# The last third of a decoder layer rearranged: norm, projections and the last feed-forward block

## The chip, the cores and the metric

One core of a Trainium2 chip runs the program. The metric is the device time of one execution in microseconds (us). PE is the matrix engine, DVE, ACT and POOL are the engines that work on vectors, and SP only issues DMAs. Each of them takes its instructions in a fixed order.

## The reference

One layer over 2048 tokens with 1024 features: eight attention heads (three dilated patterns, merged by weights from their softmax sums) beside eight RWKV-7 heads, whose 1024 outputs meet in `w_out`; then a layer norm, a SwiGLU feed-forward net with 2816 hidden features, and a second layer norm.

```python
mix = jnp.concatenate([o_att, o_rw], axis=-1) @ w_out[l]
h = layer_norm(ALPHA * h + mix, ln_mix_g[l], ln_mix_b[l])

ffn = (jax.nn.silu(h @ w_ffn_gate[l]) * (h @ w_ffn_up[l])) @ w_ffn_down[l]
h = layer_norm(ALPHA * h + ffn, ln_ffn_g[l], ln_ffn_b[l])
```

`layer_norm` subtracts the mean, divides by the standard deviation, multiplies by a vector g over the features and adds a vector b.

## The kernel before

Three parts run one after the other: `recurrent` (RWKV), `attention`, and `tail` (everything in the four lines above). The change touches `tail` and the end of `attention`, the function `merge`.

**Precision.** Every matmul of the tail runs in three parts. `split` makes a rounded copy "h" of an operand on ACT (L143), and the remainder "l" by a subtraction on DVE or POOL (L149). PE then adds h·h, l·h and h·l, each one matmul of 128x128 by 128x512.

**Merge.** For head pair 3, the last one, `merge` forms the weighted sum of three patterns in four pieces Q of 512 tokens. For Q 0 and 1 PE spreads the weights, and DVE and POOL multiply (L962, L964). For Q 2 and 3 the weights come back from DRAM (tile `f`, loads issued by POOL at L948); POOL makes two of the products, DVE the third (L950) and the last addition (L968).

**Tail.** Tokens are in four blocks of 512, numbered 0 to 3.
- `mix` projects a block by `w_out`: 8 k-steps, each with a load of weights (`draw`), a load of the heads' outputs (`or`), their splits, and 3 matmuls for each 128-token tile and each half of the 1024 columns. A block costs 192 matmuls.
- `norm_mix` normalises a block with g and b on DVE and POOL and stores it to `z_d`; `transposed` turns it by PE transposes (32 a block, tiles `tp`), copies it by ACT (`ht`) and stores it to `h_d`.
- `operands(S)` loads two blocks back (`hr`), makes differences on POOL (L1136, 16 in all) and 28 splits: the right-hand operands of a Strassen scheme with seven products, B11 to B22 and T1 to T4.
- `up(S)` runs gate and up products for 1024 tokens: 1848 matmuls into PSUM tiles `y`; results go to `hid_d`.
- `down(B)` multiplies a block's hidden features (`hraw`) by `w_ffn_down` (`draw`): 22 k-steps, 528 matmuls. `finish` is the second norm and the store of `out`.

Before, all three inputs of `product` (`draw`, `or`, `hraw`) share four slots, and `graw`, `hr`, `T`, `ht` share four others. The 8 PSUM banks are one pool. The order of the work is `mix` of blocks 0 and 1 (k 4 to 7), then the rest of 0, the rest of 1, 2 and 3, `up(0)`, `down(0)`, `down(1)`, `up(1)`, `down(2)`, `down(3)`. A generator `beside` is advanced by one step after each k-step and so lays norms, transposes and operands between the matmuls; the Tile framework then fixes each engine's order. The last block runs its k-steps three times: token tiles 0 to 2, then tile 3's left half, then its right half, so `draw` is loaded and split again for tile 3.

Of the kernel before, what the change touches and what calls it, by code (L numbers as in the profile page):

```python
# [9 lines left out]
F32 = mybir.dt.float32  # L10
F32R = mybir.dt.float32r
# [94 lines left out]
FAST = True  # L106
MIXED = (1, 2)
LASTLOW = ("pool", "pool", "dve")
# [4 lines left out]
class Layer:  # L113
# [617 lines left out]
    def attention(self):  # L731
        nc, tc, io = self.nc, self.tc, self.io
        amask = self.cst("amask")
        with ExitStack() as es:
# [160 lines left out]
            def merge(hp, os_, stats):  # L895
# [43 lines left out]
                w4 = w.rearrange("p a (h n) -> p a h n", h=2)  # L939
                for Q in range(NQ):  # L940
                    cols = slice(Q * QT, (Q + 1) * QT)
                    us = []
                    for p in range(3):
                        u = fp.tile([128, QT], F32, name="u", bufs=3)
                        if hp < 3 or Q >= NPE:
                            f = fp.tile([128, QT], F32, name="f", bufs=6)
                            src = self.f_d[hp, p, :, cols]
                            nc.gpsimd.dma_start(f, bass.AP(tensor=src.tensor, offset=src.offset,  # L948
                                                           ap=[list(src.ap[0]), [0, 64], [1, QT]]))
                            (nc.vector if p == 2 and hp == 3 else nc.gpsimd).tensor_tensor(u, os_[p][:, cols], f, op=ALU.mult)  # L950
                        else:

                            g = ps_s.tile([128, 4, 128], F32, name="g", tag="s")
                            for n in range(4):
                                for h in range(2):
                                    nc.tensor.matmul(g[64 * h:64 * h + 64, n], w4[:, p, h, 4 * Q + n:4 * Q + n + 1].to_broadcast([128, 64]),
                                                     self.ident, start=True, stop=True)
                            g = g.rearrange("p a b -> p (a b)")
                            if p == 0:
                                f = fp.tile([128, QT], F32, name="f", bufs=6)  # L960
                                nc.scalar.copy(f, g)
                                nc.gpsimd.tensor_tensor(u, os_[p][:, cols], f, op=ALU.mult)  # L962
                            else:
                                nc.vector.tensor_tensor(u, os_[p][:, cols], g, op=ALU.mult)  # L964
                        us.append(u)
                    if hp < 3 or Q >= NPE:
# [15 lines left out]

    def norm(self, sp, t, g, b, eps, mexp, fast=False):

        nc = self.nc
        st = sp.tile([128, 2, 6], F32, name="st", bufs=4)
        for i in range(2):
            nc.vector.bn_stats(st[:, i], t[:, i * 512:(i + 1) * 512])
        mv = sp.tile([128, 2], F32, name="mv", bufs=4)
        nc.vector.bn_aggr(mv, st)  # L990
        rs = sp.tile([128, 1], F32, name="rs", bufs=4)
# [10 lines left out]
    def tail(self):  # L1002
# [9 lines left out]
        with ExitStack() as es:  # L1012
# [22 lines left out]
            def bank(name):  # L1035
                return ps.tile([128, 512], F32, name=name, tag="y")
# [263 lines left out]
```

## Time and profile before

| quantity | value |
|---|---|
| time, median of 3 runs | 3450.7 us (3448.55 to 3455.49) |
| time of the profiled execution | 3452.88 us |
| its span (first to last event) | 3451.1 us |
| granted clock of PE, mean over the span | 0.943 |
| PE busy | 3202.5 us, 93% |
| tail, from its first matmul at 1729.12 us | 1722.0 us |

The span runs from the first to the last recorded event. An engine's busy share says how much of that it worked; a wait row says which engine's result ended a wait. The tail is cut into six stages below: projections, `up(0)`, `down(0)` with `down(1)`, `up(1)`, `down(2)`, `down(3)` with the end.

### The profile page before, as it was taken

Reading aid. Unit: us, or ns where it says so; the run is one execution under the profiler, and the core shown is the slowest. Engines: PE = TensorE matmul, PEld = TensorE weight load, DVE = VectorE, ACT = ScalarE, POOL = GpSimd, SP = SyncE. Lnnn points to the kernel's source line nnn. Section 1 sums busy time; section 2 is a strip of 40 time slices with the busy share of each in tenths; the row PEclk is TensorE's granted clock in tenths of the full one; section 3 lists DMA queues with packets and bytes.
Section 4 is the critical chain, followed back from the end, with each engine's and each line's share of the span. In section 5 each row is a group of like instructions: output and inputs, shape, how many; then the busy total and the mean of one; then the engine's idle time right before and its main releaser. Section 6 shows DMA issues by size and latency. Waiting matters only on the chain.

```text
span 3451.1 us, 48043 instructions
## 1 busy us (share of the span) xinstructions
PE 3202.5 (93%) x16836; PEld 2549.9 (74%) x16836; DVE 1916.0 (56%) x3887; ACT 1261.5 (37%) x2892; POOL 1294.9 (38%) x1298
## 2 busy tenths in 40 slices
PE   8999999999999988999978679999899999999996
PEld 5677778777777876777766568888777788888774
DVE  3456556566565433666547855555735655554334
ACT  4443343333332324666423423333422232323233
POOL 4444444343333240044414643232524522221286
PEclk9999999899888899999989889999999999999998
DMA  5553343443432448553347542222544322224455
GB/s 148 145 131 97 86 121 100 107 107 98 107 99 78 114 132 195 119 142 105 119 127 261 201 147 86 80 80 84 204 139 147 116 98 79 80 80 153 132 189 174
DMA packets 420317, 431.79 MB, mean 125 GB/s; under 512 B 97833, under 2 KB 313513, under 8 KB 417002
## 3 DMA queue, kind: packets, MB, share of 16 engines
q1 hardware_dynamic: 396490, 413.16, 40.0%
q0 software_dynamic: 23584, 15.56, 1.7%
q8 instruction: 132, 2.16, 0.3%
q14 instruction: 111, 0.91, 0.1%
HBM read 329.49 MB, written 98.97 MB: 124 GB/s over the span
## 4 chain that ended last, share of the span: by engine, by line
PE 48%; DMA 9%; DVE 7%; POOL 3%; issue 3%; ACT 2%; SPq 0%; ACTq 0%; POOLq 0%; DVEq 0%
PE y L1185 8%; PE y L1183 8%; PE y L1184 8%; DMA hraw<-hid_d 4%; PE acc L852 3%; PE s L812 3%; PE t L834 2%; DVE wl L149 2%; PE acc L1065 2%; PE acc L1064 2%; PE acc L1063 2%; PE s L813 2%; PE yr L291 1%; ACT wh L143 1%; PE yr L292 1%
## 5 line engine op out<-in xcount | busy, mean ns | idle before, releaser
L149 POOL TENSOR_TENSOR wrl<-wraw,wrh 128x256 fp32r<-128x256 f32 x416 | 330.1, 798 | 507.3 <-ACT wrh L143 477.8
L291 PE MATMUL yr<-xh,wrh 128*128 128x512 f32 x832 | 363.3, 437 | 48.3 <-ACT xh L143 22.5
L149 DVE TENSOR_TENSOR wl<-draw,wh 128x512 fp32r<-128x512 f32 x209 | 200.4, 980 | 324.6 <-ACT wh L143 295.1
L292 PE MATMUL yr<-xl,wrh 128*128 128x512 f32 x832 | 349.9, 421 | 0.9 <-DVE xl L149 0.8
L293 PE MATMUL yr<-xh,wrl 128*128 128x512 f32 x832 | 349.6, 421 | 1.0 <-POOL wrl L149 0.5
L143 ACT CAST wrh<-wraw 128x256 fp32r<-128x256 f32 x416 | 166.1, 404 | 442.9 <-PE yr L292 279.0
L1064 PE MATMUL acc<-wh,p 128*128 128x512 f32 x656 | 264.5, 404 | 28.8 <-DVE p L149 22.2
L1065 PE MATMUL acc<-wl,p 128*128 128x512 f32 x656 | 263.4, 405 | 4.2 <-POOL wl L149 2.7
L1063 PE MATMUL acc<-wh,p 128*128 128x512 f32 x656 | 239.4, 405 | 20.9 <-ACT p L143 19.9
L143 ACT CAST wh<-draw 128x512 fp32r<-128x512 f32 x284 | 169.7, 619 | 206.7 <-PE acc L1064 67.8
L1169 POOL TENSOR_TENSOR S<-graw 128x512 f32<-128x512 f32 x44 | 58.1, 1320 | 493.1 <-DVE gl L149 447.3
L291 PEld LDWEIGHTS yr<-xh,wrh 128*128 128x128 f32 x832 | 169.1, 203 | 97.0 <-ACT xh L143 27.2
L143 ACT CAST gh<-graw 128x512 fp32r<-128x512 f32 x176 | 109.3, 621 | 305.1 <-PE y L1184 287.0
L817 ACT ACTIVATE e<-e,ml 128x256 f32<-128x256 f32 (+1 forms) x384 | 175.0, 457 | 92.5 <-DVE ml L815 88.9
L815 DVE CUSTOM_DVE_ANT_0 e<-s,c 128x256 f32<-128x256 f32 (+1 forms) x384 | 134.2, 363 | 130.9 <-PE s L813 114.5
L293 PEld LDWEIGHTS yr<-xh,wrl 128*128 128x128 f32 x832 | 167.3, 201 | 43.0 <-POOL wrl L149 5.6
L292 PEld LDWEIGHTS yr<-xl,wrh 128*128 128x128 f32 x832 | 168.3, 202 | 38.2 <-DVE xl L149 5.1
L149 POOL TENSOR_TENSOR p<-hraw,p 128x512 fp32r<-128x512 f32 x66 | 87.8, 1332 | 288.4 <-ACT p L143 288.4
L1064 PEld LDWEIGHTS acc<-wh,p 128*128 128x128 f32 x656 | 126.7, 193 | 64.6 <-DVE p L149 25.5
L143 ACT CAST gh<-S 128x512 fp32r<-128x512 f32 x132 | 82.1, 622 | 243.6 <-PE y L1184 230.7
L1063 PEld LDWEIGHTS acc<-wh,p 128*128 128x128 f32 x656 | 127.5, 196 | 51.0 <-ACT p L143 23.7
L812 PE MATMUL s<-kh,qs 128*128 128x256 f32 (+1 forms) x384 | 162.8, 430 | 0.3 <-ACT vs L327 0.3
(450 smaller groups left out, 8227.9 us busy)
## 6 DMA issues: line engine op xcount, KB each, us to landing
draw<-w_ffn_down SPq DMA_DIRECT2D x220, 256.0 KB
wraw<-w_in SPq DMA_DIRECT2D x288, 128.0 KB
graw<-w_ffn_gate SPq DMA_DIRECT2D x44, 512.0 KB
graw<-w_ffn_up SPq DMA_DIRECT2D x44, 512.0 KB
hid_d<-c SPq DMA_DIRECT2D x44, 512.0 KB
hraw<-hid_d SPq DMA_DIRECT2D x88, 256.0 KB
xn<-x_t SPq DMA_DIRECT2D x64, 256.0 KB
wraw<-w_qk SPq DMA_DIRECT2D x128, 128.0 KB
```

The source lines that it names most:

```text
L143: nc.scalar.copy(hi, src)
L149: e.tensor_tensor(lo, src, hi.bitcast(F32), op=ALU.subtract)
L291: nc.tensor.matmul(y[:, p], wh[:, i], h[:, p], start=k == 0 and a == 0, stop=False)
L292: nc.tensor.matmul(y[:, p], wh[:, i], l[:, p], start=False, stop=False)
L293: nc.tensor.matmul(y[:, p], wl[:, i], h[:, p], start=False, stop=k == KT - 1 and a == WN - 1)
L812: nc.tensor.matmul(s[:, i, c0:], Qs[h][:, qsl], Kh[h][:, ksl], start=True, stop=False)
L1063: nc.tensor.matmul(y, h[:, tk], wh, start=k == ks[0], stop=False)
L1064: nc.tensor.matmul(y, l[:, tk], wh, start=False, stop=False)
L1065: nc.tensor.matmul(y, h[:, tk], wl, start=False, stop=k == ks[-1])
L1183: nc.tensor.matmul(y, wh[:, k], h, start=k == 0, stop=False)
L1184: nc.tensor.matmul(y, wh[:, k], l, start=False, stop=False)
L1185: nc.tensor.matmul(y, wl[:, k], h, start=False, stop=k == 3)
```

## The change

- **Merge:** for Q 2 and 3 POOL makes all products and additions of every head pair; the `f` loads of head pair 3 are written ahead of Q 0 (in POOL's order they stand behind its products of Q 0 and 1, as before).
- **Norm after the projection:** DVE only subtracts the mean and scales (`scaled`, one instruction a tile); ACT applies g and b while it copies the transposed tile. The token-major copy in `z_d` gets g and b later: blocks 0 to 2 are loaded again during `up(0)` (`completed`: load, two DVE instructions, store), block 3 after its transposes.
- **Order:** `mix(1)` runs by token pairs, with two steps of `beside` a k-step; `mix(2)` by halves with two steps. `mix(3)` moves behind `up(0)`. `operands(1)` is laid beside `down(0)`.
- **Down:** blocks 0 to 2 run by halves of the columns: 44 k-steps of 12 matmuls where there were 22 of 24, so `hraw` is loaded and split twice. Block 3 runs once over all eight PSUM banks; its last four k-steps have their operands kept, and PE finishes one (tile, half) after another, with its sum and norm behind it.
- **Memory:** `hraw` gets two slots of its own, `draw` and `or` six; `z` tiles 6 where there were 8; PSUM becomes two pools of four banks.

```diff
...
+                def weights(Q):
+                    out = []
+                    for p in range(3):
+                        f = fp.tile([128, QT], F32, name="f", bufs=6)
+                        src = self.f_d[hp, p, :, Q * QT:(Q + 1) * QT]
+                        nc.gpsimd.dma_start(f, bass.AP(tensor=src.tensor, offset=src.offset,
+                                                       ap=[list(src.ap[0]), [0, 64], [1, QT]]))
+                        out.append(f)
+                    return out
+                first = NPE if hp == 3 else 0
+                fs_ = {Q: weights(Q) for Q in range(first, NQ)} if first else {}
...
                     cols = slice(Q * QT, (Q + 1) * QT)
+                    if Q >= first:
+                        us = fs_.get(Q) or weights(Q)
+                        for p in range(3):
+                            nc.gpsimd.tensor_tensor(us[p], os_[p][:, cols], us[p], op=ALU.mult)
+                        nc.gpsimd.tensor_tensor(us[0], us[0], us[1], op=ALU.add)
+                        nc.gpsimd.tensor_tensor(us[0], us[0], us[2], op=ALU.add)
+                        nc.gpsimd.dma_start(self.o_d[hp, :, cols], us[0])
+                        continue
+
                     us = []
...
+                            nc.vector.tensor_tensor(u, os_[p][:, cols], g, op=ALU.mult)
                         us.append(u)
-                    if hp < 3 or Q >= NPE:
-                        nc.gpsimd.tensor_tensor(us[0], us[0], us[1], op=ALU.add)
-                        (nc.vector if hp == 3 else nc.gpsimd).tensor_tensor(us[0], us[0], us[2], op=ALU.add)
-                    else:
-                        nc.vector.tensor_tensor(us[1], us[1], us[2], op=ALU.add)
-                        nc.vector.tensor_tensor(us[0], us[0], us[1], op=ALU.add)
-                    nc.gpsimd.dma_start(self.o_d[hp, :, cols], us[0])
+                    nc.vector.tensor_tensor(us[1], us[1], us[2], op=ALU.add)
+                    nc.vector.tensor_tensor(us[2], us[0], us[1], op=ALU.add)
...
-            np_ = pool("tn", 8)
+            np_ = pool("tn", 6)
-            ps = pool("tps", 8, space=PSUM)
+            pa = pool("tpa", 4, space=PSUM)
+            ps = pool("tps", 4, space=PSUM)
...
-            def bank(name):
-                return ps.tile([128, 512], F32, name=name, tag="y")
+            def bank(name, a=False):
+                return (pa if a else ps).tile([128, 512], F32, name=name, tag="a" if a else "y")
+
+            def part(n, i, kk, dt=F32R):
+
+                return ip.tile([128, 2, 512], dt, name=f"{n}{i}{kk}")
...
+                for gi, (tts, halves) in enumerate(groups):
+                    acc = {q: bank("acc", i < 4 and gi % 2 == 0) for i, q in enumerate((tt, half) for tt in tts for half in halves)}
...
+                            raw = rp.tile([128, 512], F32, name="draw", bufs=6)
+                            if memory:
+                                wh, wl = memory.pop(), memory.pop()
+                            else:
+                                wh, wl = (wp.tile([128, 512], F32R, name=n) for n in ("wh", "wl"))
...
+                    now = ks[:len(ks) - held]
+                    for i, k in enumerate(now):
+                        ws = weights(k)
                         pairs = lhs(k)
+                            for half in halves:
+                                products(k, pairs, ws, tt, half)
+                        for _ in range(steps):
+                            next(beside, None)
+                        if callable(z) and i == len(now) - 6:
+                            z = z()
+                    later = [(k, lhs(k, slots), weights(k, slots)) for k in ks[len(ks) - held:]]
+                            for k, pairs, ws in later:
+                                products(k, pairs, ws, tt, half)
+                            if held:
+                                sums(tt, half)
+                    if not held:
+                        for tt in tts:
+                            for half in halves:
+                                sums(tt, half)
...
+            def scaled(z, B):
                 for tt, t in enumerate(z):
-                    self.norm(sp, t, rows["g"], rows["b"], eps, mexp, fast or tt in MIXED)
-                    nc.sync.dma_start(self.z_d[(4 * B + tt) * 128:(4 * B + tt + 1) * 128], t)
+                    nc.vector.tensor_scalar(t, t, *moments(t), op0=ALU.subtract, op1=ALU.mult)
+                    if B < 3:
+                        store(t, B, tt)
                     yield
 
+            def affine(t):
+                nc.vector.tensor_tensor(t, t, rows["g"], op=ALU.mult)
+                nc.vector.tensor_tensor(t, t, rows["b"], op=ALU.add)
+
+            def completed(Bs):
+
+                for B in Bs:
+                    for tt in range(4):
+                        t = np_.tile([128, D], F32, name="z")
+                        nc.sync.dma_start(t, self.z_d[(4 * B + tt) * 128:(4 * B + tt + 1) * 128])
+                        affine(t)
+                        store(t, B, tt)
+                        yield
...
-                    nc.scalar.copy(t, tp)
+                    nc.scalar.activation(t, tp, AF.Identity, bias=cols["b"][:, k:k + 1], scale=cols["g"][:, k:k + 1])
+                if B == 3:
+                    for tt, t in enumerate(z):
+                        affine(t)
+                        store(t, B, tt)
+                        yield
...
+            def down(B, groups, beside=iter(()), slots=None):
+                z = []
+
+                def residual():
+                    z.extend(tokens(self.z_d, B))
+                    return z
+
+                def lhs(k, memory=None):
+                    raw = rp.tile([128, 512], F32, name="hraw", bufs=2)
+                    nc.sync.dma_start(raw, self.hid_d[k, :, B * 512:B * 512 + 512])
+                    p = [memory.pop() for _ in range(2)] if memory else pair(k)
+                    self.split(raw, *p, "act", "pool")
+                    return [p]
+                end = finish(z, B)
+                product(io["w_ffn_down"][0], range(NH), lhs, residual, ALPHA, groups, beside, end if slots else None,
+                        held=4 if slots else 0, slots=slots)
+                return end
 
...
-            zs = [tokens(io["x"][0], B) for B in (0, 1)]
-            mix((0, 1), zs, [4, 5, 6, 7], ALPHA, ("T1h", "T1l", "T4h", "T4l"), groups=[(range(8), (0,)), (range(8), (1,))])
+            keep = [q + (1,) for q in early]
+            z0 = tokens(io["x"][0], 0)
+            kept = [part(*q) for q in keep[:8]]
+            first = [part(n, i, 0, F32).rearrange("p a b -> p (a b)") for n, i in early[:4]]
+            z1 = tokens(io["x"][0], 1, first)
+            mix((0, 1), (z0, z1), [4, 5, 6, 7], ALPHA, kept, groups=[(range(8), (0,)), (range(8), (1,))])
             load_rows("mix")
-            mix((0,), zs[:1], [0, 1, 2, 3], 1.0, ("T3h", "T3l"), groups=SPLIT, done=norm_mix(zs[0], 0, True))
-            tasks = transposed(zs[0], 0)
-            mix((1,), zs[1:], [0, 1, 2, 3], 1.0, ("B22h", "B22l"), groups=half, beside=tasks)
-            flush(tasks)
+            mix((0,), (z0,), [0, 1, 2, 3], 1.0, keep[8:12], groups=SPLIT, done=scaled(z0, 0))
+            mix((1,), (z1,), [0, 1, 2, 3], 1.0, [q + (0,) for q in early[4:8]], groups=SPLIT, done=scaled(z1, 1),
+                beside=transposed(z0, 0), steps=2, lows=("dve", "pool"))
             hT = {}
-            tasks = chain(norm_mix(zs[1], 1), transposed(zs[1], 1), operands(0, hT))
-            zs = []
-            for B in (2, 3):
-                zs.append(tokens(io["x"][0], B))
-                mix((B,), zs[-1:], range(KT), ALPHA, groups=half, beside=tasks, lows=("dve", "pool"))
-                if B == 2:
-                    tasks = chain(tasks, norm_mix(zs[0], 2), transposed(zs[0], 2))
-            flush(tasks)
-            tasks = chain(norm_mix(zs[1], 3), transposed(zs[1], 3))
+            tasks = chain(transposed(z1, 1), operands(0, hT))
+            z2 = tokens(io["x"][0], 2)
+            mix((2,), (z2,), range(KT), ALPHA, keep[:8], groups=half, done=scaled(z2, 2), beside=tasks, steps=2, lows=("dve", "pool"))
+            flush(tasks, transposed(z2, 2))
+            tasks = completed(range(3))
             up(0, hT, tasks)
             flush(tasks)
-            tasks = operands(1, hT)
+            z3 = tokens(io["x"][0], 3)
+            mix((3,), (z3,), range(KT), ALPHA, keep[:8], groups=half, done=scaled(z3, 3))
+            hT = {}
+            tasks = chain(transposed(z3, 3), operands(1, hT))
+            end = down(0, half, tasks)
+            flush(tasks)
             load_rows("ffn")
-            whole = [(range(4), (0, 1))]
-            for B in range(NQ):
-                if B == 2:
-                    flush(tasks)
-                    up(1, hT, iter(()))
-                z = tokens(self.z_d, B)
-                if B < NQ - 1:
-                    product(io["w_ffn_down"][0], range(NH), hidden(B), z, ALPHA, whole, tasks)
-                    tasks = chain(tasks, finish(z, B))
-                else:
-                    product(io["w_ffn_down"][0], range(NH), hidden(B, True), z, ALPHA,
-                            [((0, 1, 2), (0, 1)), ((3,), (0,)), ((3,), (1,))], tasks, finish(z, B, True), LASTLOW)
+            end = down(1, half, end)
+            flush(end)
+            up(1, hT, iter(()))
+            end = down(2, half)
+            down(3, [(range(4), (0, 1))], end, [t[:, i] for q in keep[:12] for t in (part(*q),) for i in range(2)])
```

At the end of the merge, the change moves instructions on DVE. Before (names: `u` a weighted piece, `o` a pattern's output, `T4l`/`T4h` slots that hold the split of `or`):

```order
L964 TENSOR_TENSOR u_17865<-o_17230,g_17866 128x512
L964 TENSOR_TENSOR u_17876<-o_17537,g_17877 128x512
L970 TENSOR_TENSOR u_17865<-u_17865,u_17876 128x512
L971 TENSOR_TENSOR u_17852<-u_17852,u_17865 128x512
L950 TENSOR_TENSOR u_17898<-o_17537,f_17899 128x512
L968 TENSOR_TENSOR u_17890<-u_17890,u_17898 128x512
L950 TENSOR_TENSOR u_17913<-o_17537,f_17914 128x512
L968 TENSOR_TENSOR u_17905<-u_17905,u_17913 128x512
L149 TENSOR_TENSOR T4l_17976<-or_17991,T4l_17976 128x512
```

and in the changed kernel (`B11h1` to `B21h1` are the slots that hold `or` there):

```order
L973 TENSOR_TENSOR u_17839<-o_17194,g_17840 128x512
L973 TENSOR_TENSOR u_17850<-o_17501,g_17851 128x512
L975 TENSOR_TENSOR u_17839<-u_17839,u_17850 128x512
L976 TENSOR_TENSOR u_17850<-u_17827,u_17839 128x512
L146 TENSOR_TENSOR B11h1_17928<-or_17958,B11h1_17928 128x512
L146 TENSOR_TENSOR B11l1_17929<-or_17962,B11l1_17929 128x512
```

The four instructions L950 and L968 no longer stand ahead of the tail's first splits on DVE.

Where the projections end and `up(0)` begins, PE had before the last matmuls of `mix(3)` and the first seven transposes of block 3:

```order
L1063 MATMUL acc<-wh,p_19843 128x512
L1064 MATMUL acc<-wh,p_19844 128x512
L1065 MATMUL acc<-wl,p_19843 128x512
L1113 MATMUL tp<-c,z 128x128 x7
L1183 MATMUL y<-B11h,gh 128x512
```

and has in the changed kernel the last matmuls of `mix(2)` and the transposes of block 2:

```order
L1058 MATMUL acc<-wh,T3l_18867 128x512
L1059 MATMUL acc<-wh,T3l_18867 128x512
L1060 MATMUL acc<-wl,T3l_18867 128x512
L1157 MATMUL tp<-c,z 128x128 x32
L1236 MATMUL y<-B11h_19046,gh 128x512
```

All 192 matmuls of `mix(3)` have gone from this place, and no transposes are left for `up(0)`.

At the program's end POOL had a run of splits of re-loaded weights before, one for every k-step's turn:

```order
L149 TENSOR_TENSOR wl_30735<-draw_30732,wh_30734 128x512
L149 TENSOR_TENSOR wl_30744<-draw_30741,wh_30743 128x512
L149 TENSOR_TENSOR wl_30762<-draw_30759,wh_30761 128x512
L149 TENSOR_TENSOR wl_30771<-draw_30768,wh_30770 128x512
L992 TENSOR_TENSOR rs_30783<-mv_30781,eps_17953 128x1
L993 TENSOR_TENSOR rs_30783<-rs_30783,mexp_17955 128x1
```

and has now the splits of the last hidden features, then only the norms' small steps:

```order
L146 TENSOR_TENSOR T4l1_29903<-hraw_30720,T4l1_29903 128x512
L146 TENSOR_TENSOR p1_30693<-hraw_30690,p0_30692 128x512
L146 TENSOR_TENSOR T1h1_29900<-hraw_30732,T1h1_29900 128x512
L146 TENSOR_TENSOR T2l1_29897<-hraw_30744,T2l1_29897 128x512
L146 TENSOR_TENSOR B21h1_29894<-hraw_30756,B21h1_29894 128x512
L1124 TENSOR_TENSOR rs_30799<-mv_30797,eps_17912 128x1
```

No split of weights stands on POOL there any more; those of the last block are all on DVE, once each.

## Rows read from the trace of the kernel before

**Rows 1.** Busy time by stage: PE, weight loads, DVE, ACT, POOL; PEclk, DMA, GB/s.

```profile
1729.12:1995.03 265.91, 210.09 (x865) 164.69 (x865) 191.02 (x240) 92.80 (x159) 100.16 (x75) 0.90 0.57 195
1995.03:2449.77 454.74, 436.10 (x1881) 355.77 (x1881) 257.81 (x347) 140.54 (x218) 150.04 (x106) 0.97 0.28 94
2449.77:2721.99 272.22, 254.14 (x1057) 199.45 (x1056) 139.93 (x145) 84.79 (x151) 95.20 (x67) 0.97 0.48 165
2721.99:3147.56 425.57, 423.72 (x1849) 347.36 (x1848) 251.39 (x350) 131.07 (x202) 143.97 (x102) 1.00 0.25 86
3147.56:3271.34 123.78, 123.13 (x529) 98.32 (x527) 41.09 (x44) 36.03 (x64) 27.33 (x22) 1.00 0.48 165
3271.34:3451.10 179.76, 142.36 (x529) 102.00 (x528) 70.45 (x83) 65.07 (x107) 130.80 (x100) 0.91 0.52 179
```

**Rows 2.** Waits of PE, 1705 to 1760 us: total, times, longest.

```profile
PE acc L1064 <- DVE T4l L149: 15.6, 1, 15.6
```

**Rows 3.** Timeline of DVE, end of the merge: start, length, idle before.

```profile
1741.48 0.69 DVE L950 TENSOR_TENSOR u<-o,f 128x512 f32<-128x512 f32 x1 [10.98 <-DMA o_d<-u]
...
1747.76 1.29 DVE L149 TENSOR_TENSOR T4l<-or,T4l 128x512 fp32r<-128x512 f32 x2
```

**Rows 4.** Timeline of PE, the last transposes of block 1.

```profile
1882.60 1.91 PE L1113 MATMUL tp<-c,z 128*128 128x128 f32 x16
```

**Rows 5.** Timeline of POOL: first and last subtraction of `operands(0)`.

```profile
1895.13 1.29 POOL L1136 TENSOR_TENSOR T<-hr 128x512 f32<-128x512 f32 x1
...
1946.75 1.36 POOL L1136 TENSOR_TENSOR hr<-T,hr 128x512 f32<-128x512 f32 x1
```

**Rows 6.** Busy time in 1900 to 1960 us, columns as in rows 1.

```profile
1900.00:1960.00 60.00, 35.58 (x112) 27.10 (x112) 59.38 (x59) 26.44 (x46) 43.53 (x31) 0.79 0.50 178
```

**Rows 7.** Groups of DVE in the same stretch: busy, mean ns of one.

```profile
L149 DVE TENSOR_TENSOR p<-or,p 128x512 fp32r<-128x512 f32 x10 | 14.3, 1432 | 0.0
```

**Rows 8.** Timeline of SP and ACT as `up(0)` starts.

```profile
1987.42 0.42 SPq L1161 DMA_DIRECT2D graw<-w_ffn_gate  x1
...
1994.34 0.63 ACT L143 CAST gh<-graw 128x512 fp32r<-128x512 f32 x1
```

**Rows 9.** Groups of DVE in 2200 to 2400 us, inside `up(0)`.

```profile
L149 DVE TENSOR_TENSOR gl<-S,gh 128x512 fp32r<-128x512 f32 x31 | 21.3, 687 | 15.6 <-ACT gh L143 15.6
L1204 DVE TENSOR_TENSOR c<-c 128x1024 f32<-128x1024 f32 x10 | 12.2, 1220 | 0.0
```

**Rows 10.** Timeline of PE in `down(2)`: one row is the first of three matmuls.

```profile
3192.47 0.39 PE L1063 MATMUL acc<-wh,p 128*128 128x512 f32 x1
...
3201.99 0.39 PE L1063 MATMUL acc<-wh,p 128*128 128x512 f32 x1
```

**Rows 11.** Timeline of SP and ACT in `down(0)`: loads of `hraw`, then their casts.

```profile
2506.19 0.33 SPq L1224 DMA_DIRECT2D hraw<-hid_d  x1
...
2530.72 0.33 SPq L1224 DMA_DIRECT2D hraw<-hid_d  x1
...
2510.49 0.62 ACT L143 CAST p<-hraw 128x512 fp32r<-128x512 f32 x1 [5.22 <-DMA hraw<-hid_d]
...
2533.49 0.62 ACT L143 CAST p<-hraw 128x512 fp32r<-128x512 f32 x1 [3.68 <-DMA hraw<-hid_d]
```

**Rows 12.** Timeline of ACT, POOL and DVE in one k-step of `down(2)`.

```profile
3193.43 0.62 ACT L143 CAST p<-hraw 128x512 fp32r<-128x512 f32 x1 [4.29 <-DMA hraw<-hid_d]
...
3194.13 1.29 POOL L149 TENSOR_TENSOR p<-hraw,p 128x512 fp32r<-128x512 f32 x1 [4.66 <-ACT p L143]
3194.60 1.97 DVE L149 TENSOR_TENSOR wl<-draw,wh 128x512 fp32r<-128x512 f32 x2 [3.98 <-ACT wh L143]
```

**Rows 13.** Last block, 3362 to 3443 us: waits of PE.

```profile
PE acc L1065 <- POOL wl L149: 14.6, 20, 3.5
```

**Rows 14.** The same stretch: one group of POOL.

```profile
L149 POOL TENSOR_TENSOR wl<-draw,wh 128x512 fp32r<-128x512 f32 x34 | 47.9, 1423 | 23.0 <-ACT wh L143 17.1 <-PE acc L1065 4.1 <-PE acc L1064 1.4
```

**Rows 15.** Timeline of PE, its last matmul.

```profile
3442.17 0.49 PE L1065 MATMUL acc<-wl,T4h 128*128 128x512 f32 x1 [0.28 <-POOL wl L149]
```

More of the change, by code (lines that the diff above doesn't have):

```diff
@@ L1026, in tail @@
             names = ("B11", "B21", "T2", "T3", "T1", "T4", "B22")
+            early = [(n, i) for n in names for i in "hl"]
             rows = {}
@@ L1057, in product, with sums @@
+                    def sums(tt, half):
+                        cs = slice(half * 512, half * 512 + 512)
+                        nc.vector.scalar_tensor_tensor(z[tt][:, cs], z[tt][:, cs], alpha, acc[tt, half], op0=ALU.mult, op1=ALU.add)
+                        if done and half and half == halves[-1]:
+                            next(done)
+                    now = ks[:len(ks) - held]
+                    for i, k in enumerate(now):
+                        ws = weights(k)
                         pairs = lhs(k)
@@ L1076, in tokens @@
+            def tokens(src, B, tiles=None):
                 z = []
                 for tt in range(4):
-                    t = np_.tile([128, D], F32, name="z")
+                    t = tiles[tt] if tiles else np_.tile([128, D], F32, name="z")
                     nc.sync.dma_start(t, src[(4 * B + tt) * 128:(4 * B + tt + 1) * 128])
@@ L1081, in tokens, with mix, lhs @@
                 return z
[L1083 removed]
+            def mix(Bs, zs, ks, alpha, keep, **kw):
                 kept = {}
[L1086 to L1098 removed]
+                free = [t[:, i] for q in keep for t in (part(*q) if isinstance(q, tuple) else q,) for i in range(2)]
+                def lhs(k, _=None):
+                    if k not in kept:
+                        pairs = []
+                        for B in Bs:
+                            raw = rp.tile([128, QT], F32, name="or", tag="draw", bufs=6)
+                            nc.sync.dma_start(raw, self.o_d[k, :, B * QT:(B + 1) * QT])
+                            p = [free.pop(0) for _ in range(2)]
+                            self.split(raw, *p)
+                            pairs.append(p)
@@ L1206, in up, with finish @@
                         g = g or c
-                        for _ in range(6):
-                            next(beside, None)
-            def finish(z, B, fast=False):
-                for tt, t in enumerate(z):
-                    self.norm(sp, t, rows["g"], rows["b"], eps, mexp, fast or tt in MIXED)
+                        next(beside, None)
+            def finish(z, B):
+                for tt in range(4):
+                    t = z[tt]
+                    mean, rs = moments(t)
+                    nc.vector.scalar_tensor_tensor(t, t, mean, rows["g"], op0=ALU.subtract, op1=ALU.mult)
+                    nc.vector.scalar_tensor_tensor(t, t, rs, rows["b"], op0=ALU.mult, op1=ALU.add)
```

158 lines of the change are left out of this document (55 added, 103 removed).

## The prediction

> **What bounds the kernel now.** I read the busy time by stage first [rows 1]; the reader should compare each length with PE's busy time. Where the two agree PE is the bound: `up(1)` takes 425.57 us with 423.72 busy, `down(2)` 123.78 with 123.13. Nothing can be won there without fewer matmuls, and the change leaves out none of them. Elsewhere PE stands idle: 55.8 us in the projections (265.91 - 210.09), 18.6 in `up(0)`, 18.1 in `down(0)` and `down(1)`, 37.4 in the last block. Together 130 of the tail's 1722 us, and some busy time is long because the granted clock was 0.90 to 0.97 in just these stages and 1.00 in the two full ones.
>
> Then the waits name the places. In the projections one wait of 15.6 us stands out: PE at the tail's second matmul waits for a split on DVE [rows 2]. The timeline of DVE shows why: DVE had no work for 10.98 us, since the next instruction in its order, L950, is part of the attention merge and waits for a transfer; the split that PE needs came behind it, at 1747.76 [rows 3]. The second place is 1900 to 1960 us, where DVE is busy 59.38 of 60 us, POOL 43.53 and PE only 35.58 [rows 6]: the operands of `up(0)` are made there. The third is the last block: PE waits 20 times, 14.6 us in all, for POOL's weight splits [rows 13], which are 34 of 1.423 us each [rows 14].
>
> **Prices.** A matmul at full clock: 42 of them between the two rows of `down(2)`, 9.52 us, so 0.2267 us [rows 10]. A transpose: 1.91 / 16 = 0.12 [rows 4]. A subtraction of 128x512 on DVE alone 0.687 [rows 9], beside a busy POOL 1.43 [rows 7]; on POOL 1.29 [rows 5]. The affine pass is an operation of 128x1024, 1.22 [rows 9].
>
> **Merge and projections, start to `up(0)`.** DVE's four waiting instructions go, and with them the 15.6 us; POOL does their work while PE runs the projections. Their results are needed by blocks 2 and 3 only, some 90 us later. If that cover were gone, the same 15.6 would come back later in `mix(2)`. Block 1's transposes ended at 1884.5 [rows 4]. Before they lay at k-steps 5 to 12 of `mix(2)` (one step each, four of norm first), now at 1 to 4: 8 k-steps of 12 matmuls earlier, 21.8 us. So they end at 1884.5 - 15.6 - 21.8 = 1847. From there the operands took 64 us (to 1948.1, [rows 4, 5]). Alone they need 16 subtractions on POOL (20.6) and 28 splits on DVE (19.2): 40 us if the two engines may not work at once, and the splits of `mix(2)` go on beside. But block 2's norm loses its two POOL passes and a DVE pass. I take 57, nearer the measured 64. Behind it come block 2's transposes (3.8 us), their copies, and the first gate weights, which took 6.9 us from issue to cast [rows 8]: 11. `up(0)` then starts at 1915, so the stage is 186 us (bounds 165 and 215: 40 us for the operands and 7 behind, or each of the 28 splits 0.74 dearer than I allow, and the first weights late). Of the 80 us won here, 43.5 are the 192 matmuls of `mix(3)`, which are only moved.
>
> **`up(0)`.** It loses block 3's transposes and norms and gains 24 affine instructions, 29 us of DVE, which had some 197 us free (454.74 - 257.81). It should come near `up(1)`: 425.6, and 6 for the first weight loads and for waits on `z` tiles, of which there are 6 now, while each pair of feature tiles takes six in turn: 432 (427 to 445).
>
> **`mix(3)`, `down(0)`, `down(1)`.** 192 and 1056 matmuls 282.9, 32 transposes 3.8: 286.7. On top: 6 for the change from `up(0)` into `mix(3)` and into `down(0)`. Beside `down(0)` lie 16 steps of operands, one for each k-step of 12 matmuls, 2.72 us; so 43.5 us of PE must cover 40 us of operand work, while each k-step itself wants a POOL subtraction and a DVE one, 1.98 us. In one k-step of before two DVE subtractions beside one of POOL took 1.97 us where 1.37 is their price alone [rows 12]: they do overlap only in part. Full exclusion would lack 40 + 31.7 - 43.5 = 28 us; I take 25. `down(1)`: 4. Sum 321.8 (298 if they overlap, 350 if the load loop below joins in).
>
> The Trainium skill ("SBUF — State Buffer", "Who interferes with whom") says that DVE and GpSimd share one port pair that an instruction holds as an exclusive lock, and that a DVE instruction with two SBUF inputs contends with GpSimd's reads. It speaks against splitting `hraw` twice on POOL. By it the lack is the 28, not 25, and the total 3 us more; the rows 1.43 against 0.687 agree with its direction.
>
> **`up(1)`** is unchanged work: 425.6.
>
> **`down(2)`** at 44 k-steps of 2.72 us takes 119.7. Its loads have two slots now. Before, load to cast took 4.30 and 2.77 us in the two extremes of five [rows 11], mean 3.3; from cast to the end of POOL's subtraction 1.99 (3193.43 to 3195.42, [rows 12]). A slot turns in 5.3 us, two give 2.65 a k-step: just under 2.72. With the slow load it is 3.15. I take 2.85 for the mixture: 126 (122 to 135).
>
> **`down(3)`**: 119.7 for 528 matmuls, 4 for its start, then from last matmul to the span's end 8.9 as before (3451.1 - 3442.2, [rows 15]), rounded to 10: 134 (128 to 152). The second loads, casts and POOL splits of weights for token tile 3 are gone, so the waits of [rows 13] go; the last four k-steps hold no load on PE's path. Each finished tile costs DVE two sums, two statistics and two passes, about 5.3 us by their durations, under 24 matmuls, 5.4.
>
> **Sum.** 186 + 432 + 321.8 + 425.6 + 126 + 134 = 1625.4; with 1729.1 ahead the span is 3354.5. The profiled execution took 1.8 more than its span, and the median is 2.2 less than it: 3354, 97 us or 2.8% less.
>
> **Rivals.**
> 1. *The load loop binds (slower).* Before, four shared slots served three loads in 6.13 us (four periods between the rows, 24.53, [rows 11]), so a slot was held 8.2 us. Should each of the two `hraw` slots be held as long, a k-step takes 4.09, and 132 of them 540 us where I count 394 for the three blocks: 3500. It decides from 3.72 us a k-step. For it: POOL is late in `down(0)`. Against: the slots were held by order, behind loads of weights, which now have six of their own.
> 2. *Operands dearer.* Splits of both stages at 1.43 instead of 0.687: 28 x 0.74 = 20.7 twice, 3395. For it: DVE's 59.38 of 60 [rows 6].
> 3. *Everything hides.* Projections 165, `up(0)` 427, the third stage 298: 50 less, 3304. Against: the same row.
> 4. *The end gives less.* Sums and norms by tile fall behind PE and `down(3)` takes 150: 3370.
>
> **How the numbers follow.** Forecast 0.60 (own range 3330 to 3380), rival 1 0.04, rival 2 0.17, rival 3 0.14, rival 4 0.05. The range 3310 to 3400 holds the forecast, rivals 2 and 4 and a part of 3. A measurement of this kernel tells some 0.2%, 7 us, from no change; only rival 1 is near or over the old time. Faster 0.94, same 0.02, slower 0.04.
>
> **What would show it.** In the profile after: no DVE wait over 5 us at the tail's first matmuls; the first gate product near 1915; PE's idle time in `up(0)` under 12 us; in `down(0)` waits of PE for POOL's `p`, some 25 us, in its first half above all; in `down(2)` a k-step between 2.72 and 2.9 with waits for `p`; the last matmul some 8.9 us before the end. I am wrong if casts of `hraw` in `down(2)` come 3.7 us apart, if the operands of `up(0)` end later than 1930, or if `down(3)` still shows POOL waits.

## The result

The changed kernel takes 3395.36 us (median of 4 runs, 3387.83 to 3398.84) against 3449.62 before (median of 4). The ratio is 0.9837, with a 95% interval from 0.9816 to 0.9858: 1.6% faster, some 54 to 56 us, where 97 were forecast. 3395 lies in the stated range (3310 to 3400), at its upper end.

The profiled execution took 3387.83 us, with a span of 3386.1. The tail began at 1723.9 us in it, and at 1729.1 before. That start says little of the change: over the 14 profiles of this study, whose programs differ ahead of the tail in the merge alone, it lies anywhere between 1708 and 1744. So the lengths of stages within the tail are the sharper measure. The tail was 1722.0 us, is 1662.2, and was forecast at 1625.4.

The busy time by stage of the changed kernel, the same six stages as in [rows 1]; the third now holds `mix(3)`, `down(0)` and `down(1)`:

```profile
1723.91:1918.22 194.31, 154.83 (x673) 123.40 (x673) 130.50 (x180) 76.23 (x124) 79.03 (x69) 0.89 0.63 212
1918.22:2350.38 432.16, 432.16 (x1848) 350.21 (x1849) 260.94 (x358) 135.63 (x208) 126.69 (x91) 0.99 0.34 112
2350.38:2694.31 343.93, 307.99 (x1281) 245.88 (x1280) 192.69 (x208) 133.26 (x228) 158.50 (x117) 0.94 0.62 206
2694.31:3130.45 436.14, 431.80 (x1849) 349.05 (x1848) 246.00 (x348) 131.78 (x203) 136.65 (x99) 1.00 0.26 84
3130.45:3256.50 126.05, 122.14 (x532) 99.06 (x531) 61.83 (x56) 50.83 (x88) 54.97 (x43) 1.00 0.62 205
3256.50:3386.10 129.60, 120.13 (x527) 98.37 (x525) 70.23 (x89) 35.06 (x60) 45.10 (x37) 0.98 0.45 154
```

Beside the forecast: projections 194.3 (186), `up(0)` 432.2 (432), third stage 343.9 (321.8), `up(1)` 436.1 (425.6), `down(2)` 126.1 (126), last block 129.6 (134). The excess is 8.3 + 0.2 + 22.1 + 10.5 + 0.1 - 4.4 = 36.8 us. The reader should look at the third row: PE is busy 308 of 344 us, and at a clock of 0.94.

Within it the loss is in one place. The same columns for 2420 to 2500 us, when `operands(1)` lies beside `down(0)`, and for the end of `down(1)`:

```profile
2420.00:2500.00 80.00, 54.61 (x185) 39.80 (x184) 69.43 (x59) 33.33 (x59) 52.28 (x32) 0.81 0.74 252
...
2600.00:2694.31 94.31, 92.88 (x408) 76.21 (x407) 43.19 (x43) 38.84 (x66) 42.76 (x33) 1.00 0.53 175
```

In 80 us, 185 matmuls; at 0.2267 us each they need 42. The waits of PE in those 80 us come from POOL and from ACT, both for `p`, the split of `hraw`:

```profile
PE acc L1059 <- POOL p L146: 13.0, 8, 3.0
PE acc L1058 <- ACT p L140: 12.4, 4, 7.1
```

That is 25.4 of the 38 us that are lost there. The rest is the clock, 0.81 on the mean: the matmuls keep PE busy 54.6 us instead of 42.

### The profile page after: what moved, and what is told of

Its sections match the earlier page's. It is cut to its first block, busy times and chain, and to the rows that moved or that the text cites. A ratio compares the mean times of both kernels' runs of the same rounds, so it can differ in the third digit from the quotient of the medians.

```text
span 3386.1 us, 48376 instructions
## 1 busy us (share of the span) xinstructions
PE 3172.3 (94%) x16836; PEld 2540.6 (75%) x16836; DVE 1924.8 (57%) x3918; ACT 1275.6 (38%) x2906; POOL 1247.5 (37%) x1285
## 4 chain that ended last, share of the span: by engine, by line
PE 58%; DMA 6%; DVE 5%; issue 1%; POOL 1%; ACT 1%; SPq 0%; POOLq 0%; DVEq 0%; ACTq 0%
PE y L1236 8%; PE y L1238 8%; PE y L1237 8%; PE acc L1059 5%; PE acc L1060 5%; PE acc L1058 5%; PE acc L849 4%; PE s L809 3%; PE t L831 3%; PE s L810 2%; PE yr L288 1%; PE yr L289 1%; PE yr L290 1%; DMA hraw<-hid_d 1%; DVE wl L146 1%
## 5 line engine op out<-in xcount | busy, mean ns | idle before, releaser
L146 DVE TENSOR_TENSOR wl<-draw,wh 128x512 fp32r<-128x512 f32 x224 | 219.8, 989 | 263.0 <-ACT wh L140 221.6
L146 POOL TENSOR_TENSOR p<-hraw,p 128x512 fp32r<-128x512 f32 x150 | 204.8, 1366 | 284.8 <-ACT p L140 279.0
L1059 PE MATMUL acc<-wh,p 128*128 128x512 f32 x672 | 269.7, 402 | 20.2 <-POOL p L146 20.2
L1058 PE MATMUL acc<-wh,p 128*128 128x512 f32 x672 | 209.8, 398 | 20.6 <-ACT p L140 19.7
L140 ACT CAST wh<-draw 128x512 fp32r<-128x512 f32 x240 | 147.1, 620 | 192.1 <-PE acc L1059 152.0
L1058 PEld LDWEIGHTS acc<-wh,p 128*128 128x128 f32 x672 | 127.9, 192 | 52.5 <-ACT p L140 24.1
```

The lines of the kernel that those rows point to most:

```text
L140: nc.scalar.copy(hi, src)
L146: e.tensor_tensor(lo, src, hi.bitcast(F32), op=ALU.subtract)
L1058: nc.tensor.matmul(y, h[:, tk], wh, start=k == ks[0], stop=False)
L1059: nc.tensor.matmul(y, l[:, tk], wh, start=False, stop=False)
```

## The experiments

All times are medians of four to ten runs, with the ratio to the kernel before on the same chip; stage lengths are from each run's one profile. Where kernels are alike in a stage, the lengths still differ: the third stage took 338.7 to 343.9 us in the four in which nothing touches it (the changed kernel, and those below with eight banks, the old merge and the old last block), the projections 193.4 to 199.5 in the five with six slots for `draw` and the new merge. Two explanations of the third stage were to be told apart: that DVE and POOL have too much work between 2420 and 2500 us, or that the two `hraw` slots turn too slowly.

**Affine pass later, operands spaced.** One line each:

```diff
-            tasks = chain(transposed(z3, 3), operands(1, hT))
+            tasks = chain(transposed(z3, 3), operands(1, hT), residuals(z3, 3))
```

```diff
-            tasks = chain(transposed(z3, 3), operands(1, hT))
+            tasks = chain(transposed(z3, 3), spaced(operands(1, hT)))
```

(`residuals` is the affine pass and store of z3, taken out of `transposed`; `spaced` gives an empty step behind each step.) Expected of the first:

> The affine pass of block 3 (8 DVE instructions of 128x1024, 13.8 us in the profile, and four stores of 512 KB) moves from ahead of operands(1) to behind it, still beside down(0). Theory 'DVE and POOL are overbooked' in 2420 to 2500 us: the stage from mix(3) to up(1), 343.9 us in the changed kernel, gets 8 to 14 us shorter, since the second half of down(0) has DVE idle three quarters of the time. Rival 'load loop' (two hraw slots wait for their loads): within 3 us of the changed kernel.

and of the second:

> operands(1) is laid beside down(0) at one step for every second k-step instead of each: 16 steps over 32 k-steps. Theory 'DVE and POOL are overbooked': 87 us of PE now cover the 40 us of operand work and 63 us of the k-steps' own subtractions, so the stage from mix(3) to up(1) gets 20 to 30 us shorter than 343.9. Rival 'load loop': less than 8 us shorter, the waits for p only spread out. Rival 'transfers' (DMA busy 0.9 in 2420 to 2460 us with hr, z and the stores): 5 to 15 us shorter, since the same bytes are spread as well.

Measured: 3392.67 us (0.9827, 0.9762 to 0.9893) and 3394.86 us (0.9834, 0.9786 to 0.9882); third stage 341.1 and 343.1. At first this reads as a verdict against the crowd on DVE. It isn't one. The timeline of DVE of the first shows seven of the eight affine instructions (L1139, L1140) still ahead of the first operand split (`B11l`), as in the changed kernel:

```profile
2428.18 5.73 DVE L1139 TENSOR_TENSOR z<-z,b_g 128x1024 f32<-128x1024 f32 x4 [2.21 <-PE tp L1157]
2433.84 0.68 DVE L146 TENSOR_TENSOR wl<-draw,wh 128x512 fp32r<-128x512 f32 x1
2434.44 3.44 DVE L1140 TENSOR_TENSOR z<-z,b_b 128x1024 f32<-128x1024 f32 x2
...
2439.48 2.28 DVE L1140 TENSOR_TENSOR z<-z,b_b 128x1024 f32<-128x1024 f32 x1
2441.69 1.75 DVE L146 TENSOR_TENSOR B11l<-hr,B11h 128x512 fp32r<-128x512 f32 x1
2443.36 2.30 DVE L1140 TENSOR_TENSOR z<-z,b_b 128x1024 f32<-128x1024 f32 x1
```

In the second the operands' splits on DVE keep their places too. The edits changed the text and hardly the order that the framework fixed, so these two runs decide nothing.

**Four slots for `hraw`.**

```diff
-                            raw = rp.tile([128, 512], F32, name="draw", bufs=6)
+                            raw = rp.tile([128, 512], F32, name="draw", bufs=4)
...
-                    raw = rp.tile([128, 512], F32, name="hraw", bufs=2)
+                    raw = rp.tile([128, 512], F32, name="hraw", bufs=4)
```

> hraw gets four slots instead of two, draw and or four instead of six. Rival 'load loop': the stage from mix(3) to up(1) gets 20 us or more shorter, and down(2), 126.0 us, falls to 121. Theory 'DVE and POOL are overbooked': the third stage changes by less than 6 us, the waits of PE for POOL's p in 2420 to 2500 us remain; down(2) at most 3 us shorter.

Measured: 3376.69 us (0.978, 0.9734 to 0.9826). The third stage is 319.8 us, 24.1 shorter (18.9 under the shortest of the four alike), with PE's busy time down by 9 at a clock of 0.98; the projections are 209.1, 14.8 longer. `down(2)` alone, from its first matmul to the first of the last block, falls from 125.4 to 122.6; the last block is 1.5 longer. So the loop of the loads cost some 24 us in the third stage and 3 in `down(2)`, where nothing else is laid beside it. And six slots for `draw` and `or` are worth 10 to 16 us in the projections.

**One ring of eight slots.**

```diff
-                            raw = rp.tile([128, 512], F32, name="draw", bufs=6)
+                            raw = rp.tile([128, 512], F32, name="draw", bufs=8)
...
-                    raw = rp.tile([128, 512], F32, name="hraw", bufs=2)
+                    raw = rp.tile([128, 512], F32, name="hraw", tag="draw", bufs=8)
```

> hraw, draw and or share one ring of eight slots, the same memory as six and two. With four hraw slots and four of the others the third stage had fallen from 343.9 to 319.8 us and the projections had grown from 194.3 to 209.1. Theory 'load loop': what counts is how many loads of each kind are under way, so the projections are back at 194 to 198 us, the third stage stays at 318 to 326, and the time is 3355 to 3368. Rival: in a shared ring a late hraw holds up the weights behind it, as before the change, and the third stage is back above 335.

Measured: 3361.36 us (0.9735, 0.9704 to 0.9767), 34 us under the changed kernel in the same memory; its tail is 1632.1 us, 30 shorter. (The interval of the ratio overlaps that of four and four slots; there the stages tell them apart.) Both gains are there: its projections and its third stage, columns as above:

```profile
1731.50:1925.70 194.20, 153.56 (x673) 123.85 (x673) 130.54 (x179) 74.07 (x121) 81.01 (x69) 0.89 0.63 211
2356.60:2673.40 316.80, 299.00 (x1282) 240.76 (x1281) 184.15 (x206) 130.85 (x228) 167.27 (x120) 0.97 0.65 218
```

The waits of PE in its 2400 to 2520 us:

```profile
PE acc L1060 <- DVE wl L146: 6.9, 3, 4.6
PE acc L1059 <- POOL p L146: 4.7, 5, 1.6
PE acc L1058 <- ACT p L140: 2.3, 2, 1.5
```

The waits for `p` have fallen from 25.4 to 7.0 us, and a wait for DVE's weight split has come up.

**The ring, and then DVE relieved.** Two kernels put the edits of above on top of the ring.

> The shared ring of eight slots, and block 3's affine pass behind operands(1). With the ring the third stage took 316.8 us, 30 over its matmuls and transposes, and DVE was busy 20.00 of 20 us from 2440 to 2500. Theory 'loop first, DVE second': now that the loads are early, DVE's 13.8 us of affine work count, and the third stage falls by 6 to 12 us, where the same edit without the ring gave 2.8. Rival: the crowd is only shifted (block 0's and 1's norms and the affine pass meet later) and the stage stays within 3 us of 316.8.

> The shared ring, the affine pass behind operands(1), and operands(1) at one step for every second k-step. Theory 'loop first, DVE second': spread over 87 us of PE, the operands no longer fill DVE; the third stage falls to 300 to 308 us, where the same spacing without the ring gave 0.8. Rival: no more than 3 us below the run with the affine pass alone.

Measured: 3363.79 (0.9771, 0.9742 to 0.9801) and 3367.13 us (0.9774, 0.9741 to 0.9807); third stage 316.4 and 314.9, as the rivals have it. But in both the affine pass stood ahead of the operands again, in the order of the ring alone, and they decide as little as before. A third kernel forces it: block 3's pass runs beside `up(1)`, behind a new load of g and b, so that no order can put it earlier.

```diff
-                    if B < 3:
-                        store(t, B, tt)
+                    store(t, B, tt)
...
-            up(1, hT, iter(()))
+            load_rows("mix")
+            tasks = completed((3,))
+            up(1, hT, tasks)
+            flush(tasks)
+            load_rows("ffn")
```

> The shared ring of eight slots, and block 3 treated as the other blocks: z3 is stored as scaled, and loaded again, multiplied by g, increased by b and stored beside up(1); the rows of g and b are loaded again around up(1). The two earlier tries to move the affine pass and to spread the operands changed the text but not DVE's order in the trace (the eight instructions still ran ahead of the operands), so they tested nothing; here DVE's order has the eight behind down(1). Theory 'DVE second': the third stage falls from 316.8 to 302 to 310 us, up(1) grows by at most 3, the time is 3345 to 3358. Rival 'transfers or the ring set it': the third stage stays over 313 and the time at 3358 or more.

Measured: 3354.37 us (0.9736, 0.9708 to 0.9764). Its third stage:

```profile
2349.10:2664.00 314.90, 296.36 (x1281) 240.87 (x1280) 168.03 (x197) 131.61 (x228) 165.23 (x120) 0.97 0.64 216
```

DVE has 16 us less to do there, and the stage is 1.9 us shorter, less than alike stages differ. So the affine pass, which the prediction had forgotten in this stage, isn't what sets its length once the loads are early. The stage stays over 313, as the rival has it; the time, 3354, lies in the other's range, but by its ratio this kernel is level with the ring alone. Its waits for `p` have grown again (2395 to 2480 us):

```profile
PE acc L1059 <- POOL p L146: 8.2, 3, 3.9
PE acc L1058 <- ACT p L140: 4.8, 1, 4.8
```

**The merge, undone and alone.** The old function `merge` in the changed kernel, and the new one in the kernel before.

```diff
-                            nc.gpsimd.tensor_tensor(us[p], os_[p][:, cols], us[p], op=ALU.mult)
...
+                            (nc.vector if p == 2 and hp == 3 else nc.gpsimd).tensor_tensor(u, os_[p][:, cols], f, op=ALU.mult)
```

> The changed kernel with the old merge (DVE makes the third product and the last addition of Q 2 and 3, f loads behind Q 1). By the prediction's term the wait of 15.6 us at the tail's second matmul comes back and the time is 13 to 18 us over that of the changed kernel. Rival 'the cover would come in the same place': the projections end no later, since their end is set by the operands of block 1, and the time is within 5 us.

> The kernel before with the new merge alone. If the wait of 15.6 us at the tail's second matmul is on the path, the projections fall from 265.9 to 248 to 253 us and the whole time by 12 to 17 us. Rival: the chain of operands behind it absorbs it, since DVE and POOL are full from 1900 to 1960 us; the projections stay over 260.

Measured: undone, 3405.53 us (0.9869, 0.9827 to 0.9912), 10 over the changed kernel by the medians, under the 13 to 18 expected and with an interval that overlaps its. The projections are 212.7, 18.4 longer. Alone, 3430.10 us (0.996, 0.994 to 0.9981), 13 less than before, projections 251.5, 14.4 under those of before: both as expected. The wait of PE in the first:

```profile
PE acc L1051 <- DVE B11h L146: 13.6, 1, 13.6
```

The two lie on either side of the 15.6 us that [rows 2] shows; the chain of operands doesn't absorb it. (The tail with the merge undone is 1677.8, longer by 15.6 to the tenth; that is chance, for its third stage, which the edit leaves alone, came out 5.2 shorter.)

**The last block as before.**

```diff
-            down(3, [(range(4), (0, 1))], end, ...)
+            last(3, [((0, 1, 2), (0, 1)), ((3,), (0,)), ((3,), (1,))], end, free)
```

(`last` keeps all splits of `hraw` and splits weights on POOL, POOL and DVE in turn.)

> The changed kernel with the last block as before: token tiles 0 to 2, then tile 3 by halves, with weights loaded and split again on POOL, POOL and DVE in turn. By the prediction's term (179.8 us before, 129.6 in the changed kernel) the time rises by 40 to 52 us, with waits of PE for POOL's wl again. Rival: most of the old length came from two draw slots too few; with six slots of its own draw is early enough and the time rises by less than 25 us.

Measured: 3423.66 us (0.9926, 0.9903 to 0.9948), so 28 us over the changed kernel by the medians; `down(2)` with the last block takes 290.7 us against 255.7, 35.0 more, of which the last block itself has 32. PE's waits for POOL and POOL's group of splits, as in [rows 13, 14], are back; both from 3340 to 3440 us:

```profile
PE acc L1060 <- POOL wl L146: 9.5, 16, 1.4
```

```profile
L146 POOL TENSOR_TENSOR wl<-draw,wh 128x512 fp32r<-128x512 f32 x42 | 60.3, 1455 | 20.1 <-ACT wh L140 11.2 <-PE acc L1059 8.8
```

It falls between the two expectations: most of the 50 us that the last block gained are the three passes, and some 18 are left for the slots and the rest, which no run takes apart.

**The matmuls of `up`.** Two kernels ask why `up(1)` grew.

```diff
-                            y = bank("y")
+                            turn[0] += 1
+                            y = bank("y", turn[0] % 2 == 0)
```

> The product tiles y of the two up stages take turns over both PSUM pools, so eight banks as before the change instead of four; nothing else differs. In the changed kernel up(1) took 436.1 us against 425.6 before, and 80 us in its middle hold 346 matmuls against 351. Theory 'banks': the matmul price in the middle of up(1) goes back from 0.231 to 0.228 us, and the two up stages together get 10 to 14 us shorter; the wait of 3.8 us at the start of up(1) goes as well. Rival 'operand tiles' (the operands now lie in tiles of half the size): the price stays at 0.231 and the time within 4 us of the changed kernel.

> The kernel before, with each operand tile of 128x4x512 replaced by two of 128x2x512, as the changed kernel has them; the work and its order in the code are the same. Theory 'operand tiles': 80 us in the middle of up(1) hold 345 matmuls, as in the changed kernel, and not 351; up(1) takes 432 or more. Rival 'something else in up' (6 z tiles, other addresses): 351 stay and up(1) takes 425 to 428.

(The second edits the kernel before: each `ip.tile([128, 4, 512])` becomes two of `[128, 2, 512]`.) Measured: 3395.48 us (0.9835, 0.9785 to 0.9884) and, one run, 3450.67 us. `up(1)` takes 433.6 and 425.5. One stretch of 80 us inside `up(1)`, of the kernel before, of the changed one, of the run with eight banks and of the run with half tiles, each a view of its own:

```profile
2797.68:2877.68 80.00, 80.00 (x351) 65.75 (x350) 44.26 (x64) 24.20 (x37) 22.37 (x16) 1.00 0.24 80
```

```profile
2770.00:2850.00 80.00, 80.00 (x346) 64.84 (x345) 42.79 (x62) 24.20 (x37) 23.14 (x17) 1.00 0.25 80
```

```profile
2760.00:2840.00 80.00, 80.00 (x344) 64.36 (x343) 42.98 (x62) 24.02 (x37) 22.57 (x17) 1.00 0.26 84
```

```profile
2800.00:2880.00 80.00, 80.00 (x351) 65.67 (x350) 43.56 (x62) 24.70 (x38) 23.17 (x17) 1.00 0.27 88
```

By these counts each matmul takes 0.231 us instead of 0.228, with no wait between them and the clock at 1.00. Neither the number of banks nor the size of the operand tiles does it. With eight banks `up(1)` was 2.5 us shorter: a wait of 3.8 us for DVE at its start was gone, the price was not.

## Why the prediction came out as it did

**Merge and projections: right in mechanism, 8 us short.** The wait of 15.6 us at the tail's second matmul is gone, and undoing the merge brought 13.6 of it back. `up(0)` started at 1918.2 us, 3 later than forecast, in a tail that began 5 earlier. "So they end at ... 1847" is the step that was off: I placed block 1's transposes by the generator's steps, at k-steps 5 to 12 before and 1 to 4 now, 96 matmuls earlier. In the traces 484 matmuls of the projections stand ahead of the last of them before and 466 now, so they moved by 18 matmuls, 4 us and not 21.8. They end 128.7 us after the tail's start, not 118. The chain behind them was faster than I took it (1852.6 to 1899.4, the end of POOL's last subtraction: 47 us, not 57), and what follows slower: 19 us, not 11. In it PE has its longest wait of the tail, for DVE, whose scaling of block 2 stands behind 26 of the operands' 28 splits:

```profile
PE tp L1157 <- DVE z L1133: 23.4, 2, 22.6
PE acc L1058 <- DVE u L973: 8.2, 1, 8.2
```

The second row lies just ahead of the tail: its first matmul waits for the merge's last product on DVE, 8.2 us now and 5.4 before. My sign, no DVE wait over 5 us there, didn't hold for it. After the transposes the first gate weights share slots with the `ht` copies, and SP issues them behind the stores of these, at 1912.96:

```profile
1905.79 6.66 SPq L1160 DMA_DIRECT2D h_d<-ht  x7
1912.96 0.38 SPq L1214 DMA_DIRECT2D graw<-w_ffn_gate  x1
```

**`up(0)`: right number, wrong reason.** PE is busy all 432.16 us. The 6 us that I added for waits aren't waits; the matmuls themselves cost more, as in `up(1)`. There 10.5 us were missing from the forecast: some 6.4 by this price (1848 matmuls at 0.0035 more from start to start), most of the rest by one wait of 3.8 for DVE while block 1's norm runs. "`up(1)` is unchanged work" was true, and its time changed. What raises the price stays open.

**The third stage: the step that failed.** The sum laid the loss on the subtractions of DVE and POOL ("Full exclusion would lack 28 us; I take 25") and put the load loop at nothing; the loop stood only in the bound of 350 and in rival 1. The measured excess over matmuls and transposes is 57 us (343.9 - 286.7), where the sum had 35. Of the 57, 24 to 27 went when `hraw` got more slots, without any work taken from DVE or POOL; when 16 us of DVE's work were taken away as well, 1.9 went. So the term that was missing is the load loop, rival 1's mechanism, which I had priced for three blocks at once and given 0.04. With the ring the stage takes 316.8 us, near the 321.8 of the sum. The sign that I had named, some 25 us of waits for `p`, came to the number (25.4), but it could not tell the two explanations apart: both end in that wait. My own number shows why it could strike in `down(0)`: two slots at 2.65 us a k-step against 2.72, with nothing to spare, so whatever lengthens a turn goes onto the path. The timelines of SP, ACT and POOL in the changed kernel show a turn in the crowd:

```profile
2443.99 0.39 SPq L1280 DMA_DIRECT2D hraw<-hid_d  x1
...
2449.16 0.39 SPq L1280 DMA_DIRECT2D hraw<-hid_d  x1
...
2456.71 0.32 SPq L1280 DMA_DIRECT2D hraw<-hid_d  x1
...
2449.53 0.62 ACT L140 CAST wh<-draw 128x512 fp32r<-128x512 f32 x1 [2.87 <-PE acc L1059]
...
2451.62 0.61 ACT L140 CAST p<-hraw 128x512 fp32r<-128x512 f32 x1
...
2454.97 1.71 POOL L146 TENSOR_TENSOR p<-hraw,p 128x512 fp32r<-128x512 f32 x1
```

One slot is loaded at 2443.99, cast at 2451.62 behind operand casts and a cast that waited for PE, subtracted until 2456.68, and loaded again at 2456.71: 12.7 us, 6.4 a k-step from two slots. In this turn the operands matter by where they stand in ACT's and POOL's order; no run tests that by itself.

A second part of the same loop is a transfer. As `operands(1)` ends, SP issues the first weights of `up(1)`, 512 KB each, two of them just ahead of a `hraw`. That `hraw` is cast 10 us after its issue, and PE waits 7.10 us:

```profile
2481.91 0.38 SPq L1214 DMA_DIRECT2D graw<-w_ffn_gate  x1
2482.38 0.46 SPq L1214 DMA_DIRECT2D graw<-w_ffn_up  x1
2482.95 0.44 SPq L1280 DMA_DIRECT2D hraw<-hid_d  x1
...
2493.02 0.62 ACT L140 CAST p<-hraw 128x512 fp32r<-128x512 f32 x1 [7.88 <-DMA hraw<-hid_d]
...
2494.73 1.65 PE L1058 MATMUL acc<-wh,p 128*128 128x512 f32 x3 [7.10 <-ACT p L140]
```

That the weight loads delay it is read from their place and size; it was not tried by itself. With the ring, 28 to 30 us over the matmuls and transposes remain. What sets those stays open: DVE's affine pass doesn't, and the spacing of the operands couldn't be tested, for the order didn't follow the text. The transfers are a rival that no run tried: in 2440 to 2460 us the DMA engines are busy 0.96 in the changed kernel, and 0.94 with the ring.

The rows on DVE and POOL agree with the direction of the rule on the shared port pair (the Trainium skill, "SBUF — State Buffer", "Who interferes with whom"), which the prediction weighed: a split on DVE takes 0.68 us alone and 1.75 beside POOL. The 24 us went with no subtraction moved to another engine; a part in them the rule can have only by the turn above, where POOL's subtraction took 1.71 us instead of 1.29, and no run tests that.

**`down(2)` and the last block.** The table cuts 0.7 us into the last block, whose first matmul is at 3255.82; so `down(2)` takes 125.4 us, 2.85 a k-step, the forecast to the digit. The mechanism held too: the five other kernels with two slots took 128.1 to 130.4, the five with more 122.6 or 122.7, near the 119.7 of the matmuls, so the two slots cost 3 to 8 us here. The last block gained 50 us, not 46: in its row PE waits once, for 0.7 us, and the last matmul starts 9 us before the span ends:

```profile
PE acc L1058 <- DVE z L1064: 0.7, 1, 0.7
```

**The rivals.** Rival 1 came true where `operands(1)` lies beside, at about a sixth of its price (24 to 27 of 145 us). Rival 2's time, 3395, is the measured one, but by luck: its premise came in part (the 28 splits took 1.12 us each for `up(0)` and 1.25 for `up(1)`, instead of 0.687), yet the operands of `up(0)` took 10 us less than forecast, and in the third stage it was slots that gave 24 us back. Rivals 3 and 4 didn't come.

## What to carry to other kernels

A loop of loads whose turn just fits the time of a step has no slack, and the first stage that puts other work into its engines' queues pays for it; count slots for the crowded stage, and pool them (one ring of eight beat six and two by 34 us). A sign that two explanations share can come true to the number and decide nothing. Where a scheduler sets the order, read a step's place from the listing of the order or the trace, for prediction and experiment alike: in four kernels here the text moved and the instructions hardly did. Compare stages of the part that changed, when the part ahead of it varies by more than the effect.

## What the runs showed of the hardware

The 1700 us ahead of the tail, whose program hardly differs between the runs, took 1708 to 1744 us. The same matmul in `up` took 0.228 us in the kernels built on the one before and 0.231 to 0.233 in those built on the changed one, at the same granted clock of 1.00.

DVE's subtraction of 128x512 takes 0.68 us alone and up to 1.8 beside POOL: of the 625 splits on DVE in the tail of the changed kernel 446 took under 0.75 us, 42 over 1.65, the others lie between. The timeline of DVE there:

```profile
2438.91 0.68 DVE L146 TENSOR_TENSOR B22l<-hr,B22h 128x512 fp32r<-128x512 f32 x1
2439.51 1.75 DVE L146 TENSOR_TENSOR wl<-draw,wh 128x512 fp32r<-128x512 f32 x1
2441.19 1.75 DVE L146 TENSOR_TENSOR T2l<-T,T2h 128x512 fp32r<-128x512 f32 x1
2442.86 0.68 DVE L146 TENSOR_TENSOR wl<-draw,wh 128x512 fp32r<-128x512 f32 x1
```

Where POOL's subtractions run beside it (1.71 and 1.73 us instead of 1.29) it takes 1.75, at a pitch of 1.68. With the other engine idle, one follows another after 0.60 us on DVE and after 1.25 on POOL. So a pair of one each costs 1.7 us, not much under the 1.85 that the two would cost in turns.
